# Opening a fused multiply and GELU on its large rows: one load queue, rows of 63 and 60 KB

## The chip, the cores and the metric

The kernel runs on one NeuronCore of a Trainium2 chip. A core has compute engines with an instruction stream each (here VectorE and ScalarE compute, SyncE and ScalarE issue transfers), an on-chip memory of 128 partitions, and 16 DMA engines that move data between that memory and DRAM. The metric is the device time of one execution in microseconds; lower is better.

## The reference

Two float32 arrays of 1024 x 4096 are multiplied, and the tanh form of GELU is taken of the product:

```
z = x * y
return (0.5 * z * (1 + np.tanh(np.sqrt(2 / np.pi) * (z + 0.044715 * z ** 3))))
```

Every element is read once from each of x and y and written once to the output: 3 x 16.78 MB.

## The kernel before

The work is elementwise, so the arrays are taken flat. 4,194,304 elements are 128 partitions x 32768 columns of float32. PIECES cuts the columns into three: [0, 1280), [1280, 17664) and [17664, 32768), which are rows of 5 KB, 64 KB and 59 KB in each partition. A piece is one contiguous stretch of DRAM, and each partition's row is a contiguous part of that stretch (`columns`). Each array so moves in three transfers of 128 rows, 8 rows to each of the 16 DMA engines.

x is loaded into `xs`, which has room for all of it. y is loaded into `ys`, which has room for 20440 columns; Y_LOADS lists y's loads in order, with the column of `ys` where each begins. The second load writes over part of the first one's place, so it waits until three multiplies are done (Y_FREE); the third waits for four.

VectorE multiplies in place, xs = xs * ys, in steps of at most 4096 columns (STEPS); ScalarE then applies GELU in place to the same columns. `sem_mul` and `sem_act` count their steps. Pieces are computed in the order 64 KB, 59 KB, 5 KB, and stored in the same order, each by one transfer once ScalarE is through with it. The first store also waits until y's second load has landed.

All orders are written out by hand. SyncE issues all transfers but one, in program order, and waits in between; each engine that issues has its own DMA queue (q1 is SyncE's, q10 ScalarE's). `_hoist` moves an issue ahead of the program's common start, so that it goes out at once. Before the change two loads are hoisted: x's 5 KB rows on SyncE and x's 64 KB rows on ScalarE. SyncE then waits for the 5 KB rows to land (line 81) before it issues y's 64 KB rows and x's 59 KB rows; ScalarE waits for them too (line 89) before it begins its part.

Of the kernel before, what the change touches and what calls it, by code (L numbers as in the profile page):

```python
# [1 line left out]

# [4 lines left out]


F32 = mybir.dt.float32
GELU = mybir.ActivationFunctionType.Gelu_apprx_tanh  # L10

PIECES = [(0, 1280), (1280, 17664), (17664, 32768)]

Y_LOADS = [(1280, 17664, 4056), (17664, 32768, 0), (0, 1280, 15104)]

Y_FREE = [0, 3, 4]

STEPS = [[4096] * 4, [2048] * 7 + [768], [1280]]  # L20
STORES = [(1280, 17664), (17664, 32768), (0, 1280)]
Y_BUF = 20440


def _hoist(nc, issued):

    here = nc.cur_bb.bb.instructions
    first = nc.main_func.blocks[0].instructions
    for ins in issued:
        del here[next(k for k, i in enumerate(here) if i is ins or i.name == ins.name)]  # L30
    engine = issued[0].engine
    at = next(
        k
        for k, i in enumerate(first)
        if i.engine == engine and type(i).__name__ == "InstDrain"
    )
    first[at:at] = issued


@with_exitstack  # L40
def kernel(
    ctx: ExitStack,
    tc: tile.TileContext,
    x: bass.AP,
    y: bass.AP,
    out: bass.AP,
):
    nc = tc.nc
    P = nc.NUM_PARTITIONS

    def columns(t, a, b):

        flat = t.flatten_outer_dims().rearrange("r c -> (r c)")
        pa, pb = next(q for q in PIECES if q[0] <= a and b <= q[1])
        return flat[P * pa : P * pb].rearrange("(p c) -> p c", p=P)[:, a - pa : b - pa]


    tc.close()
    tc.compile()

    xs = nc.alloc_sbuf_tensor("xs", [P, PIECES[-1][1]], F32).ap()
    ys = nc.alloc_sbuf_tensor("ys", [P, Y_BUF], F32).ap()
    sem_x = [nc.alloc_semaphore(f"sem_x{i}") for i in range(len(PIECES))]
    sem_y = [nc.alloc_semaphore(f"sem_y{i}") for i in range(len(Y_LOADS))]
    sem_mul = nc.alloc_semaphore("sem_mul")
    sem_act = nc.alloc_semaphore("sem_act")
    sem_o = [nc.alloc_semaphore(f"sem_o{i}") for i in range(len(STORES))]

    def load_x(i, engine=nc.sync):
        a, b = PIECES[i]  # L70
        return engine.dma_start(out=xs[:, a:b], in_=columns(x, a, b)).then_inc(sem_x[i], 16)

    def load_y(i):
        a, b, r = Y_LOADS[i]
        return nc.sync.dma_start(
            out=ys[:, r : r + b - a], in_=columns(y, a, b)
        ).then_inc(sem_y[i], 16)

    _hoist(nc, [load_x(0).ins])
    _hoist(nc, [load_x(1, nc.scalar).ins])  # L80
    nc.sync.wait_ge(sem_x[0], 16)
    load_y(0)
    load_x(2)
    for i in range(1, len(Y_LOADS)):
        if Y_FREE[i]:
            nc.sync.wait_ge(sem_mul, Y_FREE[i])
        load_y(i)

    nc.scalar.wait_ge(sem_x[0], 16)
    n = 0  # L90
    done = {}
    for i, (a, b, r) in enumerate(Y_LOADS):
        for j, (xa, xb) in enumerate(PIECES):
            if xa <= a < xb:
                nc.vector.wait_ge(sem_x[j], 16)
        nc.vector.wait_ge(sem_y[i], 16)  # L96
        c = a
        for w in STEPS[i]:
            nc.vector.tensor_mul(  # L99
                out=xs[:, c : c + w],  # L100
                in0=xs[:, c : c + w],
                in1=ys[:, r + c - a : r + c - a + w],
            ).then_inc(sem_mul, 1)
            n += 1
            done[c + w] = n
            nc.scalar.wait_ge(sem_mul, n)
            nc.scalar.activation(  # L107
                out=xs[:, c : c + w], in_=xs[:, c : c + w], func=GELU
            ).then_inc(sem_act, 1)
            c += w  # L110

    for i, (a, b) in enumerate(STORES):
        if i == 0:
            nc.sync.wait_ge(sem_y[-2], 16)
        nc.sync.wait_ge(sem_act, done[b])
        nc.sync.dma_start(out=columns(out, a, b), in_=xs[:, a:b]).then_inc(sem_o[i], 16)
    for i in range(len(STORES) - 1):
        nc.sync.wait_ge(sem_o[i], 16)
    nums = sorted(s.num for s in [*sem_x, *sem_y, *sem_o[:-1], sem_mul, sem_act])
    assert nums == list(range(nums[0], nums[-1] + 1))  # L120
    nc.sync.sem_clear(range(nums[0], nums[-1] + 1))
    nc.sync.wait_ge(sem_o[-1], 16).then_inc(sem_o[-1], -16)


# [1 line left out]
_INS = ['x', 'y']  # L126
_OUTS = [((1024, 4096), 'float32')]


# [23 lines left out]
```

## Time and profile before

| what | value |
|---|---|
| median of 3 runs | 119.9 us (119.77 to 119.95) |
| the profiled execution: its span, from first to last instruction | 118.5 us (a time of its own beside the span is not recorded) |
| VectorE busy, 13 multiplies | 35.2 us (30%) |
| ScalarE busy, 13 activations and a table load | 30.9 us (26%) |
| packets of the DMA engines, q1 and q10 | 82.3% and 16.5% of the 16 engines' span |
| x's 5 KB rows: issued at, time to landing | 0.00 us, 13.6 us (SyncE) |
| x's 64 KB rows | 0.12 us, 30.4 us (ScalarE) |
| y's 64 KB rows | 13.57 us, 29.0 us |
| x's 59 KB rows | 13.96 us, 46.5 us |
| y's 59 KB rows | 55.79 us, 22.5 us |
| stores of 64, 59 and 5 KB rows: time to landing | 20.9, 20.4 and 20.8 us |

The DMA share of a stretch is the mean busy share of the 16 DMA engines, from the durations of their packets; a packet counts in the stretch where it begins, so a short stretch can show more than 1. One row is one packet, and each transfer adds 16 small ones that signal its completion. The chain that ended last follows the work back from the last instruction, at each step to what released it. A transfer's time to landing includes its time in the queue behind others.

### The profile page before, as it was taken

The numbers are of one execution on the slowest core, as the hardware profiler recorded it, in microseconds if no ns is written. First come the engines' busy times: TensorE is split into PE (matmuls) and PEld (weight loads), VectorE is DVE, ScalarE is ACT, GpSimd is POOL, SyncE is SP. The second block draws the span as 40 slices with busy tenths as digits, with TensorE's granted clock in tenths as the row PEclk, the third lists the DMA queues.
The fourth block names the chain that finished last, engine by engine and source line by source line (L and its number), as shares of the span: only waits on it lengthen the run. The fifth ranks groups of instructions, "written<-read, shape, count | busy, mean of one in ns | idle before, by whom it ended". The sixth has DMA issues, their size and how long they took to land.

```text
span 118.5 us, 83 instructions
## 1 busy us (share of the span) xinstructions
DVE 35.2 (30%) x13; ACT 30.9 (26%) x14; POOL 0.2 (0%) x4
## 2 busy tenths in 40 slices
DVE  0000000000000069999920000059999940000000
ACT  0000000000000000999975000006998990000000
POOL 0000000000000000000000000000000000000000
DMA  9888899889988897798797797798899887977975
GB/s 492 382 382 382 354 597 464 354 354 465 597 354 354 354 632 347 326 632 347 326 632 347 326 632 347 326 575 354 354 531 531 354 354 326 653 326 326 653 326 221
DMA packets 1296, 50.33 MB, mean 425 GB/s; under 512 B 144, under 2 KB 144, under 8 KB 528
## 3 DMA queue, kind: packets, MB, share of 16 engines
q1 hardware_dynamic: 1152, 41.94, 82.3%
q10 hardware_dynamic: 144, 8.39, 16.5%
HBM read 33.55 MB, written 16.78 MB: 425 GB/s over the span
## 4 chain that ended last, share of the span: by engine, by line
DMA 55%; DVE 24%; ACT 3%; issue 1%; DVEq 0%
DMA ys<-in_y_dram 43%; DVE xs L99 24%; DMA xs<-in_x_dram 11%; ACT xs L107 3%; DVEq L96 0%
## 5 line engine op out<-in xcount | busy, mean ns | idle before, releaser
L99 DVE TENSOR_TENSOR xs<-xs,ys 128x2048 f32<-128x2048 f32 (+3 forms) x13 | 35.2, 2778 | 60.9 <-DMA ys<-in_y_dram 60.9
L107 ACT ACTIVATE xs<-xs 128x2048 f32<-128x2048 f32 (+3 forms) x13 | 29.6, 2300 | 19.6 <-DVE xs L99 19.6
L107 ACT ACT_TABLE_LOAD x1 | 1.3, 1283 | 47.2 <-DVE xs L99 47.2
L137 POOL MEMSET const-uint8-127<- 128x1 uint8 x1 | 0.1, 102 | 0.0
L137 POOL MEMSET const-bfloat16-1.0<- 128x1 bf16 x1 | 0.1, 101 | 0.0
L137 POOL MEMSET const-float32-0.0<- 128x1 f32 x1 | 0.1, 98 | 0.2 <-issue 0.2
L137 POOL MEMSET const-float32-1.0<- 128x1 f32 x1 | 0.1, 98 | 0.0
## 6 DMA issues: line engine op xcount, KB each, us to landing
xs<-in_x_dram SPq DMA_DIRECT2D x1, 7552.0 KB, 46.5
ys<-in_y_dram SPq DMA_DIRECT2D x1, 7552.0 KB, 22.5
out_dram<-xs SPq DMA_DIRECT2D x1, 7552.0 KB, 20.4
xs<-in_x_dram SPq DMA_DIRECT2D x1, 640.0 KB, 13.6
ys<-in_y_dram SPq DMA_DIRECT2D x1, 640.0 KB, 19.7
out_dram<-xs SPq DMA_DIRECT2D x1, 640.0 KB, 20.8
xs<-in_x_dram ACTq DMA_DIRECT2D x1, 30.4
ys<-in_y_dram SPq DMA_DIRECT2D x1, 29.0
```

What stands on the lines that cost most here:

```text
L99: nc.vector.tensor_mul(out=xs[:, c : c + w], in0=xs[:, c : c + w], in1=ys[:, r + c - a : r + c - a + w],).then_inc(sem_mul, 1)
L107: nc.scalar.activation(out=xs[:, c : c + w], in_=xs[:, c : c + w], func=GELU).then_inc(sem_act, 1)
L137: nc = _bacc.Bacc("TRN2", target_bir_lowering=False, num_devices=1)
```

## The change

The cut between the two large pieces moves from column 17664 to 17408: rows of 63 KB and 60 KB take the place of 64 KB and 59 KB, in loads, steps and stores. The second load of y still waits for three multiplies. The first piece's last step becomes 3840 columns; the second piece's last step of 768 becomes two, 640 and 384.

Only x's 63 KB rows are hoisted, on SyncE. ScalarE issues no transfer any more. SyncE does not wait before y's first load: behind the hoisted load it issues y's 63 KB rows, x's 60 KB rows and x's 5 KB rows. ScalarE waits for x's 63 KB rows where it waited for the 5 KB rows.

```
-PIECES = [(0, 1280), (1280, 17664), (17664, 32768)]
+PIECES = [(0, 1280), (1280, 17408), (17408, 32768)]
 
-Y_LOADS = [(1280, 17664, 4056), (17664, 32768, 0), (0, 1280, 15104)]
+Y_LOADS = [(1280, 17408, 4312), (17408, 32768, 0), (0, 1280, 15360)]
 
 Y_FREE = [0, 3, 4]
 
-STEPS = [[4096] * 4, [2048] * 7 + [768], [1280]]
-STORES = [(1280, 17664), (17664, 32768), (0, 1280)]
+STEPS = [[4096] * 3 + [3840], [2048] * 7 + [640, 384], [1280]]
+STORES = [(1280, 17408), (17408, 32768), (0, 1280)]
...
-    _hoist(nc, [load_x(0).ins])
-    _hoist(nc, [load_x(1, nc.scalar).ins])
-    nc.sync.wait_ge(sem_x[0], 16)
+    _hoist(nc, [load_x(1).ins])
     load_y(0)
     load_x(2)
+    load_x(0)
     for i in range(1, len(Y_LOADS)):
         if Y_FREE[i]:
             nc.sync.wait_ge(sem_mul, Y_FREE[i])
         load_y(i)
 
-    nc.scalar.wait_ge(sem_x[0], 16)
+    nc.scalar.wait_ge(sem_x[1], 16)
```

## The prediction

> **What bounds the kernel now.** I read the page's DMA rows first, then the chain that ended last, then the DMA queues over short stretches, then SyncE's waits.
>
> ```profile
> span 118.5 us, 83 instructions
> ...
> DVE 35.2 (30%) x13; ACT 30.9 (26%) x14; POOL 0.2 (0%) x4
> ...
> DMA packets 1296, 50.33 MB, mean 425 GB/s; under 512 B 144, under 2 KB 144, under 8 KB 528
> ...
> q1 hardware_dynamic: 1152, 41.94, 82.3%
> q10 hardware_dynamic: 144, 8.39, 16.5%
> ```
>
> The two queues add to 98.8% of 16 engines' span: the 16 DMA engines work for 117.1 of 118.5 us, VectorE and ScalarE for less than a third. So the transfers are the bound, and compute matters only where a transfer waits for it. The bytes, the 1152 rows and the 144 completion packets (9 transfers x 16) stay the same after the change. What is left to win or lose is engine time outside the steady rate, and that I look for by stretches. The next four fences are the DMA view over 3 to 11, 100 to 116, 0 to 2 and 0 to 3 us (packets, MB, share of 16 engines).
>
> ```profile
> q10 hardware_dynamic: 48, 3.15, 90.7%
> q1 hardware_dynamic: 48, 0.25, 7.6%
> ```
>
> ```profile
> q1 hardware_dynamic: 112, 6.77, 97.7%
> ```
>
> ```profile
> q1 hardware_dynamic: 54, 0.28, 49.0%
> ```
>
> ```profile
> q10 hardware_dynamic: 16, 1.05, 85.9%
> q1 hardware_dynamic: 80, 0.41, 43.3%
> ```
>
> Steady: a 64 KB row takes 0.907 x 8 us x 16 / 48 = 2.419 us (27.09 KB/us, with 65.536 KB), a 59 KB row 0.977 x 16 x 16 / 112 = 2.233 us (27.06 KB/us), a 5 KB row 0.076 x 8 x 16 / 48 = 0.20 us. So time goes by bytes, and row length costs nothing that shows. Opening: a 5 KB row takes 0.433 x 3 x 16 / 80 = 0.260 us and the first sixteen 64 KB rows 0.859 x 3 x 16 / 16 = 2.577 us. Over the steady rows that is 80 x 0.060 / 16 = 0.30 us, and 16 x 0.158 / 16 = 0.16 us, of every engine: 0.46 us together. And before any row:
>
> ```profile
> 0.00:1.00 1.00, 0.00 (x0) 0.00 (x0) 0.20 (x4) 1.00 0.00 0
> 1.00:2.00 1.00, 0.00 (x0) 0.00 (x0) 0.00 (x0) 1.00 0.98 276
> ```
>
> Nothing moves in the first 1.0 us (last column, GB/s); in the second the engines are busy (0.98) but move 276 GB/s, not some 430. The opening is the one place where busy engines are slow. The chain and SyncE's waits tell where the transfers depend on compute:
>
> ```profile
> 0.00 13.56 DMA xs<-in_x_dram
> ...
> 13.57 28.99 DMA ys<-in_y_dram
> ...
> 42.66 13.11 DVE xs L99 x3
> ...
> 55.79 22.46 DMA ys<-in_y_dram
> ...
> 78.34 1.52 DVE xs L99
> ...
> 80.55 13.31 DVE xs L99 x6
> ...
> 93.88 3.80 ACT xs L107 x3
> ```
>
> ```profile
> SPq L75 <- DVE xs L99: 45.4, 2, 41.4
> ...
> SPq L116 <- ACT xs L107: 18.7, 2, 17.9
> SPq L116 <- DMA ys<-in_y_dram: 14.5, 1, 14.5
> ```
>
> These waits are not engine idle time: while SyncE waits, earlier transfers run. The third y transfer covers the turn from loads to stores.
>
> **The change part by part.**
>
> *Row lengths.* 63 KB costs 2.419 x 63/64 = 2.381 us, 60 KB 2.233 x 60/59 = 2.271 us. Per engine and array: 8 x (2.381 + 2.271) = 37.22 now, 8 x (2.419 + 2.233) = 37.22 before. Zero.
>
> *Order and queue of the loads.* Before, 640 KB of x on SyncE's queue and 64 KB rows on ScalarE's interleave from about 2 us on. After, one queue holds x's 63 KB rows, y's 63 KB rows, x's 60 KB rows, x's 5 KB rows. A single queue loses nothing in the steady stretch: the 59 KB rows of 100 to 116 us are on one queue and go at full rate.
>
> *SyncE's wait for x's first piece (12.1 us) goes.* y's first load is issued at about 1.4 us instead of 13.57. Late next would be the queue's next transfer, and it isn't: before, 64 KB rows of x ran until 30.5 us (0.12 + 30.4), so y's issue was covered by 17 us; now it is covered by 8 x 2.38 = 19 us. An issue takes 0.33 to 0.43 us in the timeline; four in a row on SyncE end some 1.5 us after they begin, behind those 19 us, so zero; uncovered, the issue moved from ScalarE would cost its 0.36 us. The Trainium skill speaks against merging here (DMA: Bandwidth & Descriptors, Issuing engines are not separate DMA queues): issuing from several engines saves the sequencer's issue time, and nothing else. The saving given up is those 0.36 us and by this trace they lie under 19 us of rows, so by the rule and by the rows the sum is the same.
>
> *ScalarE now waits for x's 63 KB piece.* That lands near 20.5 us; behind the wait stand the table load and the first activation, which need the first multiply (47.17 us before). Zero.
>
> *The opening.* It now has no 5 KB rows. The 0.30 us of their slowness goes; unknown is what the first 63 KB rows cost cold. Low end: nothing above steady (gain 0.46). High end: both costs fall on the first row, and on the slowest engine, which sets each landing (in the trace's packet records single 5 KB rows reach 0.756 us against 0.196, single 64 KB ones 2.858 against 2.418, so 0.56 + 0.44 = 1.0 us, where the mean is 0.46): a loss of up to 0.5. I take the 0.16 us that the first 64 KB rows showed themselves, the same kind of transfer and nearest in time. Gain 0.30 us. The first data are put at 1.0 us after the issue, as now. High end for that: in the stretches above, the 64 KB rows of ScalarE's queue, issued at 0.12 us, have not begun at 2.0 us and all sixteen begin before 3.0. I take 1.0, because the store of 64 KB rows on SyncE's queue, issued at 78.27, has its first packet record at 79.11, 0.84 us later: large rows as such need no 2 us.
>
> *The second half of the loads.* y's first piece lands at 42.56 - 8 x 0.20 (x's 5 KB rows go behind) - 16 x 0.038 (1 KB less on 16 rows) - 0.30 = 40.05. Three multiplies of 13.11 us in total end at 53.3, and SyncE issues y's second load. The queue then still holds x's 60 KB and 5 KB rows until 40.05 + 8 x 2.271 + 1.6 = 59.8: 6.5 us of cover (before 55.8 against 60.4, 4.6). The third y load waits for the fourth multiply (3840 wide, about 4.1 us): 57.4, covered too.
>
> *The steps of the second piece.* 768 becomes 640 + 384: 256 more columns and one more instruction. From the rows 128x4096 (4420 ns) and 128x2048 (2286 ns) VectorE takes 1.042 ns a column; the pitch of 2.20 us between 2048-wide steps leaves 66 ns fixed. 640 + 384 take 1.20 us for 0.87. ScalarE (3612 and 1910 ns) follows: its last step is done 0.35 us later, and the second store is issued at 96.9 instead of 96.55 (both less the gain). The first store's rows end at about 98.5 on the earliest engine (packet records), less 0.3 for 63 KB; 96.9 + 0.84 = 97.74 is before 98.2. Hidden by 0.4 to 0.7 us; uncovered, it costs at most the 0.35.
>
> **Sum.** 118.5 - 0.30 = 118.2 us of span. The median of the runs, 119.9, stands 1.4 us above the span, which shows nothing of it; I keep it: 119.6 us (-0.25%).
>
> **The rivals.**
> 1. *The opening cost belongs to the moment, not to the rows:* until about 2.4 us the memory path is slow whatever it moves. For it: both the 5 KB and the first 64 KB rows are slow, and after that nothing is, not even y's first rows. Against: some 64 KB rows began at the steady 2.418. Then 0.46 stays: 119.9.
> 2. *Slower: large rows open badly.* The 5 KB rows are a cheap warm-up; the first 63 KB row of the latest engine takes both cold costs, and every landing waits for that engine. From where its lag exceeds today's it decides: +0.25 to +0.5, 120.15 to 120.4. Or the first data come at 2.1 us as ScalarE's rows did: +1.1 - 0.3 = +0.8, 120.7. For it: those 2 us; against: the store's 0.84 us.
> 3. *Faster by more:* the opening is at the steady rate and the engines start level: -0.46 to -0.7, 119.2 to 119.4. For it: y's first rows in the load phase show no excess. The Trainium skill (same page, Latency and other measured facts) tells of large power-of-two row pitches in HBM that cost rate, tabulated from 512 KiB up; leaving 64 KB would then help throughout. The trace does not agree: 27.09 against 27.06 KB/us for 64 and 59 KB rows.
> 4. *The second store is late,* if a step on ScalarE costs 0.5 us more than worked out: at most +0.35 on a gain of 0.30: 119.95.
>
> **How the numbers follow.** The runs spread 119.77 to 119.95, so 0.2% (0.24 us) is about what can be told. Forecast 0.48 (0.38 of it past -0.2%, 0.10 short of it); rival 1 0.17, no difference; rival 2 0.23, slower; rival 3 0.09, faster; rival 4 0.03, no difference. Faster 0.47, same 0.30, slower 0.23. The range runs from 119.2 (rival 3's lower part left out) to 120.3 (the late first data left out); the forecast's own is 119.4 to 119.75.
>
> **What would show it.** In the profile after: in the DMA view of the first 3 us only q1, no 5 KB rows, 16 to 32 rows; their mean against 2.381 us is the cold cost (forecast 0.16, rival 1 0.46, rival 2 more). No packet before 1.0 us, and the first soon after. y's first landing near 40.05, its second near 77.95, stores of 20.8 us to landing, the second store's issue before 97.3 and no slack before its rows. A steady row off 27.1 KB/us, or an engine idle between 53 and 60 or at 98 us, makes the prediction wrong.

## The result and the profile after

The changed kernel takes 120.37 us (median of 5 runs, 120.28 to 120.44) against 119.78 us (5 runs beside them; the 119.9 that the forecast starts from is the median of three). The ratio is 1.0047, with a 95% interval of 1.0036 to 1.0059: slower by about half a per cent. The forecast was 119.6 us, faster, with a range up to 120.3. Rival 2, slower because large rows open badly, had named 120.15 to 120.4.

The profiled execution took 120.29 us, and its span is 119.0 us; 1.3 us lie around the span, as before. From the page after, the span and the DMA rows:

```profile
span 119.0 us, 85 instructions
...
DMA packets 1296, 50.33 MB, mean 423 GB/s; under 512 B 144, under 2 KB 144, under 8 KB 528
...
q1 hardware_dynamic: 1296, 50.33, 98.5%
```

Packets and bytes are the same, all on one queue, and the engines are busy for nearly the same share (98.8% before) of a span that is 0.5 us longer. The chain that ended last (start, duration, what) tells by when that half microsecond is lost:

```profile
1.45 39.36 DMA ys<-in_y_dram
...
40.91 13.11 DVE xs L98 x3
...
54.04 24.66 DMA ys<-in_y_dram
...
94.33 4.11 ACT xs L106 x4
```

y's second load lands at 54.04 + 24.66 = 78.70, against 78.25 before: 0.45 us late. y's first lands at 1.45 + 39.36 = 40.81. Without any change of the opening it would have landed at 42.56 - 1.60 - 0.61 = 40.35 (x's 5 KB rows moved behind it, 1 KB less on 16 rows), so there too it is 0.46 late. The whole loss is there by then, and what follows only carries it along. The opening, in the DMA view of 0 to 3 us (packets, MB, share of 16 engines):

```profile
q1 hardware_dynamic: 16, 1.03, 101.2%
```

and, for a steady row, the same view from 4.8 to 20 us:

```profile
q1 hardware_dynamic: 96, 6.19, 94.0%
```

A first row takes 1.012 x 3 x 16 / 16 = 3.036 us; a steady one 0.940 x 15.2 x 16 / 96 = 2.381 us, to the nanosecond what was worked out. So the first row of an engine costs on average 0.655 us more than its bytes. From the second row on there is no excess (2.384 us, packet records). Before, the 5 KB rows and first 64 KB rows together cost 0.46, so the rows themselves make 0.20 of the loss.

Most of the rest is that the engines begin later. In the packet records the first packet stands at 1.02 us, as before. But the 16 engines begin their first rows between 1.02 and 2.04, on average at 1.28; before, all of them had begun by about 1.3, on average at about 1.11. (The records do not name the engine; which packet follows which is read from their times.) That is about 0.17 us. What is left, some 0.1, lies between the engines' mean and the landing. That a landing waits for the latest engine explains little of the loss: from the first engine to the last, y's first piece ends within 0.69 us after the change (39.74 to 40.43) and within 0.68 before (41.55 to 42.23).

### The profile page after: what moved, and what is told of

Its sections match the earlier page's. It is cut to its first block, busy times and chain, and to the rows that moved or that the text cites. A ratio compares the mean times of both kernels' runs of the same rounds, so it can differ in the third digit from the quotient of the medians.

```text
span 119.0 us, 85 instructions
## 1 busy us (share of the span) xinstructions
DVE 35.3 (30%) x14; ACT 31.0 (26%) x15; POOL 0.2 (0%) x4
## 2 busy tenths in 40 slices
DMA packets 1296, 50.33 MB, mean 423 GB/s; under 512 B 144, under 2 KB 144, under 8 KB 528
## 3 DMA queue, kind: packets, MB, share of 16 engines
q1 hardware_dynamic: 1296, 50.33, 98.5%
## 4 chain that ended last, share of the span: by engine, by line
DMA 54%; DVE 23%; ACT 3%; issue 1%; DVEq 0%
DMA ys<-in_y_dram 54%; DVE xs L98 23%; ACT xs L106 3%; DVEq L95 0%
## 5 line engine op out<-in xcount | busy, mean ns | idle before, releaser
L98 DVE TENSOR_TENSOR xs<-xs,ys 128x2048 f32<-128x2048 f32 (+5 forms) x14 | 35.3, 2591 | 61.6 <-DMA ys<-in_y_dram 61.6
L106 ACT ACTIVATE xs<-xs 128x2048 f32<-128x2048 f32 (+5 forms) x14 | 29.7, 2149 | 22.0 <-DVE xs L98 22.0
```

Source lines behind the costliest of these rows:

```text
L98: nc.vector.tensor_mul(out=xs[:, c : c + w], in0=xs[:, c : c + w], in1=ys[:, r + c - a : r + c - a + w],).then_inc(sem_mul, 1)
L106: nc.scalar.activation(out=xs[:, c : c + w], in_=xs[:, c : c + w], func=GELU).then_inc(sem_act, 1)
```

## Experiments: which part of the change costs

Each run is compared with runs of the kernel before on the same chip; ratios are to it. From group to group the kernel before took 119.74 to 119.92 us, so across groups the ratios compare better than the times. Three theories: the opening costs (theory 1, by the size of its rows or by the lack of a second queue), or the row lengths do.

**The old opening with the new cut.**

```
-    _hoist(nc, [load_x(1).ins])
+    _hoist(nc, [load_x(0).ins])
+    _hoist(nc, [load_x(1, nc.scalar).ins])
+    nc.sync.wait_ge(sem_x[0], 16)
...
-    load_x(0)
...
-    nc.scalar.wait_ge(sem_x[1], 16)
+    nc.scalar.wait_ge(sem_x[0], 16)
```

> The opening of before (5 KB rows of x on SyncE, large rows of x on ScalarE, SyncE's wait) with the new cut of 63 and 60 KB. Theory 1, the opening alone makes the difference: the time of before, 119.8 us (119.65 to 119.95), first sixteen large rows near 2.54 us. Rival, row lengths or the split last step cost it: about 120.35 us, with steady rows off 27.1 KB/us or the second store late.

119.83 us, ratio 1.0006 (0.9997 to 1.0014): no difference from before. Cut, split step and stores cost nothing; the first sixteen 63 KB rows, behind the 5 KB rows, take 0.810 x 3 = 2.43 us, less than the 2.54 expected. The DMA view of 0 to 3 us:

```profile
q10 hardware_dynamic: 16, 1.03, 81.0%
```

**The new opening with the old cut.**

```
-PIECES = [(0, 1280), (1280, 17408), (17408, 32768)]
+PIECES = [(0, 1280), (1280, 17664), (17664, 32768)]
...
-STEPS = [[4096] * 3 + [3840], [2048] * 7 + [640, 384], [1280]]
+STEPS = [[4096] * 4, [2048] * 7 + [768], [1280]]
```

(Y_LOADS and STORES go with it.)

> The opening and the single load queue of after, with the cut of before (64 and 59 KB). Theory 1: as slow as after, 120.35 us (120.2 to 120.5), first sixteen rows near 3.0 us against 2.42 steady. Rival (row lengths): 119.8 us.

120.17 us, ratio 1.0033 (1.0020 to 1.0046): slow, though 0.03 under the expected stretch. The first sixteen rows take 1.015 x 3 = 3.045 us against 2.42. The opening makes the difference. The same view:

```profile
q1 hardware_dynamic: 16, 1.05, 101.5%
```

**Small rows first, on one queue** (e3 in later expectations).

```
-    _hoist(nc, [load_x(1).ins])
+    _hoist(nc, [load_x(0).ins, load_x(1).ins])
...
-    load_x(0)
```

> After, with x's 5 KB rows issued ahead of its 63 KB rows, both on SyncE: small rows first, but one queue and no wait. Theory 1a, the size of the first rows costs: 119.8 us or a little less (119.6 to 119.9), first 5 KB rows near 0.26 us, first 63 KB rows near 2.5. Theory 1b, the missing second queue costs (ScalarE's queue): about 120.3 us, with the excess of the first 63 KB rows near 0.6 us.

119.66 us, ratio 0.9993 (0.9984 to 1.0002). The first 63 KB rows take 2.425 us behind the 5 KB rows (packet records). So neither the second queue nor SyncE's wait was worth anything that shows; the order is what counts. The Trainium skill (DMA: Bandwidth & Descriptors, Issuing engines are not separate DMA queues) says that issuing from several engines only saves issue time. The runs agree: with the same cut, two queues take 119.83 and one 119.66 us.

**Large rows first, from ScalarE.**

```
-    _hoist(nc, [load_x(1).ins])
+    _hoist(nc, [load_x(1, nc.scalar).ins])
```

> After, with the opening 63 KB rows issued by ScalarE instead of SyncE, which issues all the rest: two queues, large rows first. Theory 1a (size of the first rows): 120.35 us (120.2 to 120.6), first sixteen rows near 3.0 us. Theory 1b (queue): 119.8 us. If ScalarE's queue itself begins late, as its rows did before (no packet by 2.0 us): about 1 us more than after, 121.3 us.

120.56 us, ratio 1.0065 (1.0052 to 1.0077). First rows of 3.16 us: another queue opens no better. Its first packet comes at 1.14 us, so ScalarE's queue is not late by itself. Before, with the 5 KB load issued 0.12 us ahead of it, its rows began only at 2.23 us; why was not tried.

## Experiments: what about the first rows costs

**5 KB rows that lie 63 KB apart.** `load_part(i, c0, c1)` loads columns c0 to c1 of piece i.

```
-    _hoist(nc, [load_x(1).ins])
+    _hoist(nc, [load_part(1, 0, 1280).ins, load_part(1, 1280, 16128).ins])
```

> After, with the 63 KB rows opened by their first 5 KB (128 rows of 5 KB, 63 KB apart in DRAM) and the other 58 KB behind, all on SyncE. Theory S (the size of the rows that are begun cold costs): as with x's own 5 KB rows first, 119.7 us (119.55 to 119.9), 5 KB rows near 0.24 us. Rival P (the place: rows 63 KB apart spread the cold start over 8 MB, x's own 5 KB rows lie together in 640 KB): 120.2 to 120.4 us, with 5 KB rows well over 0.3 us.

120.03 us, ratio 1.0016 (1.0007 to 1.0026): between the two theories. (The profiled execution was the longest of its nine, 120.35 us.) The DMA view of the first 2 us shows it better; first this run, then the run with x's own 5 KB rows first, on one queue:

```profile
q1 hardware_dynamic: 27, 0.14, 43.4%
```

```profile
q1 hardware_dynamic: 66, 0.34, 48.5%
```

A 5 KB row takes 0.434 x 2 x 16 / 27 = 0.51 us when the rows lie 63 KB apart, and 0.485 x 2 x 16 / 66 = 0.24 us when they lie one behind the other. Same size, other place. Size alone cannot be the cause. The first sixteen far rows take 0.68 us, 0.49 over steady; the 58 KB rows that follow them on busy engines are steady at 2.19 (packet records).

**512 B rows first** (e6 in later expectations).

```
-    _hoist(nc, [load_x(1).ins])
+    _hoist(nc, [load_part(0, 0, 128).ins, load_x(1).ins])
...
-    load_x(0)
+    load_part(0, 128, 1280)
```

> After, with 512 B rows (the first 128 columns of x's 5 KB rows) issued ahead of the 63 KB rows on SyncE. Theory W (each engine's first packet pays once for waking up, whatever its size, so a tiny one pays cheaply): 119.7 us, first 63 KB rows under 2.45 us. Theory T (for some 1 us after its first data the path is slow, and a large row begun in that time loses more than small ones do): the tiny rows are through too soon, 120.0 to 120.3 us, first 63 KB rows 2.7 us or more.

120.78 us, ratio 1.0075 (1.0061 to 1.0089), slower than the change itself (1.0047). The tiny rows take 0.03 us and protect nothing: the 63 KB rows behind them, begun at 1.5 to 2.7 us, take 3.22 us (packet records). The last tiny packet ends at 1.57 us, so most engines are idle again before their 63 KB row. That an engine pays once for waking up, with its first packet, is not so, or it does not outlast this idle time; theory W falls as written. Theory T's bound for the first rows holds, but its time was too low by 0.5.

**The opening in two parts, 16 KB first.**

```
-    _hoist(nc, [load_x(1).ins])
+    _hoist(nc, [load_part(1, 0, 4096).ins, load_part(1, 4096, 16128).ins])
```

> After, with the 63 KB rows opened by their first 16 KB and the other 47 KB behind, on SyncE. A 16 KB row takes 0.60 us when steady, so each engine begins two of them in the first microsecond. If the loss grows with row size: between 119.75 and 120.2 us. If any row well under 63 KB does as well as 5 KB: 119.7. If place decides (rival P): 120.3.

119.96 us, ratio 1.0012 (1.0003 to 1.0021). The first sixteen 16 KB rows take 1.17 us against 0.61 steady: 0.56 over, for a quarter of the bytes, where whole 63 KB rows are 0.66 over. The excess is nearly the same for 5 (0.49), 16 and 63 KB rows at the same places; it isn't proportional to size. So the time lies in the stretch of the first theory, but the rows do not bear it out, and rival P's 120.3 is missed by 0.34. At nearly the same excess the time is less than with whole 63 KB rows while the engines keep closer together: they end y's first piece at 39.92 us on average (40.00 after), but the latest at 40.18 (40.43).

**The opening not hoisted.**

```
-    _hoist(nc, [load_x(1).ins])
+    load_x(1)
```

> After, with the opening load issued at its place in the program, about 1.4 us later, not hoisted. If the slow path belongs to the first use of it: all of the 1.4 us is added, 121.7 us, and the first sixteen 63 KB rows still take about 3.0 us. If it belongs to the time since the program's start (the path is up by about 2.4 us whoever uses it): the first rows are steady, 2.4 us, and the time is 121.0 to 121.2.

121.85 us, ratio 1.0169 (1.0155 to 1.0183). The first rows begin at 2.4 to 2.9 us and take 1.063 x 3 = 3.19 us, by the DMA view of 0 to 3 us:

```profile
q1 hardware_dynamic: 16, 1.03, 106.3%
```

The cost goes with the first use, not with the time since the program's start. That was the prediction's rival 1, and it falls.

**Large rows that lie 5 KB apart.** `load_near(i, pitch)` reads piece i's rows from the start of x, `pitch` elements apart.

```
-    _hoist(nc, [load_x(1).ins])
+    _hoist(nc, [load_near(1, 1280).ins])
```

> After, with the opening 63 KB rows read from places 5 KB apart, overlapping, all within 700 KB of x, instead of 63 KB apart over 8 MB. It moves the same bytes, but the middle columns of x get the wrong data, so this part of the product is not computed. Theory P (place: the first touch of stretches that lie far apart costs each engine): first sixteen rows 2.5 us or less, 119.6 to 119.85 us. Theory S (large rows are slow when begun cold, wherever they lie): first sixteen rows near 3.0 us, 120.2 to 120.5 us. If reading the same bytes from several engines slows the later rows too, steady rows over 2.39 us will show it.

119.82 us, ratio 0.9995 (0.9986 to 1.0004): 63 KB rows first, nothing ahead, and no slower than before. In the DMA view of 0 to 3 us of this run

```profile
q1 hardware_dynamic: 16, 1.03, 89.5%
```

is 0.895 x 3 x 16 / 16 = 2.685 us a row, 0.35 less than after. Second rows are 0.11 over steady on average (up to 0.28), later ones almost none. All engines begin by 1.30 us, as they did before and not after. The expected 2.5 us was missed, the time was hit. The four openings side by side, as ratios to before:

| | rows one near the other (5 KB apart) | rows 63 KB apart |
|---|---|---|
| 5 KB rows first | 0.9993 | 1.0016 |
| 63 KB rows first | 0.9995 | 1.0047 |

In time, where the rows lie makes the first difference, and size shows only for rows far apart. (The upper right run has one transfer more than the others.)

**2.5 KB rows first.**

```
-    _hoist(nc, [load_x(1).ins])
+    _hoist(nc, [load_part(0, 0, 640).ins, load_x(1).ins])
...
-    load_x(0)
+    load_part(0, 640, 1280)
```

> After, with half of x's 5 KB rows (2.5 KB rows, 5 KB apart) ahead of the 63 KB rows on SyncE, the other half behind. Eight of them are about 0.85 us of work for each engine, against 1.6 us for 5 KB rows and 0.2 to 0.3 us for the 512 B rows. Theory H (the first touch of the far stretches takes a fixed time of about 1 us per engine and is begun early, behind whatever work is queued ahead, so the excess that shows is what this work doesn't cover: 0.84 us behind 0.25, 0.05 behind 1.6): first 63 KB rows 2.5 to 2.8 us, 119.9 to 120.3 us. Rival T (what decides is that no large row begins in the first us): first rows begin near 2 us; by e6, whose rows that began at 2.3 and 2.7 us still took 2.75 us, they would take 2.75 or more: 120.4 or more.

120.17 us, ratio 1.0023 (1.0012 to 1.0034). The 63 KB rows behind take 2.55 us, 0.17 over steady. With 512 B rows ahead it was 0.84, with 5 KB rows 0.045: the more work is queued ahead, the less of the cost shows, as theory H says. Rival T's 2.75 did not come.

**512 B rows at the far places first.**

```
-    _hoist(nc, [load_x(1).ins])
+    _hoist(nc, [load_part(1, 0, 128).ins, load_part(1, 128, 16128).ins])
```

> After, with the first 512 B of each 63 KB row ahead of the other 62.5 KB, on SyncE. Theory P/H (first touch of the place): the tiny rows take the cost, their first ones 0.4 us or more each, the 62.5 KB rows behind run near their steady 2.36 us, 119.9 to 120.4 us in all. Theory S (size): the tiny rows are quick as in e6 (0.03 us), the large ones behind cost 0.6 to 0.9 us over steady, 120.5 to 120.9 us.

120.81 us, ratio 1.0070 (1.0056 to 1.0084). The tiny rows again take 0.03 us, and the 62.5 KB rows behind them 3.23 us against 2.36. This was a miss for theories P and H as written: reading the first 512 B of each far row beforehand doesn't pay the cost of the row. A first touch of the place where a row begins is not what costs. As with 512 B rows of x's first piece, the tiny rows are through (1.56 us) before most of the large ones begin (1.52 to 2.29).

**Small rows first on one queue, old cut.** The edit of the small-first run on the cut of before.

> Small rows first on one queue, as e3, with the cut of before (64 and 59 KB). If the cut costs nothing: as e3, 119.66 us (119.55 to 119.8), at or just under before. If the 64 KB rows do better or worse behind 5 KB rows in one queue: off that by over 0.15 us.

119.75 us, ratio 0.9986 (0.9977 to 0.9995), so 0.05 to 0.23% under before. Its interval lies under 1, by a margin that hardly counts, and under that of the change (1.0036 to 1.0059). With the new cut the same order came to 0.9993, and its interval includes 1. The first 64 KB rows take 2.53 us here, 0.11 over steady, so what is left of the cost behind 5 KB rows is not always as little as 0.045.

**Small rows landed, then large ones.** Still open: do the near rows bring the path up, or do they only cover the cost, that is, keep it from showing while they are queued ahead?

```
-    _hoist(nc, [load_x(1).ins])
+    _hoist(nc, [load_x(0).ins])
+    nc.sync.wait_ge(sem_x[0], 16)
+    load_x(1)
     load_y(0)
     load_x(2)
-    load_x(0)
```

> After, with x's 5 KB rows hoisted, and SyncE waiting until they have landed before it issues the 63 KB rows: near rows first as in e3, but nothing of the far rows can be begun behind them, and the engines stand idle in between for some 1.5 us. Theory U (the near rows bring the path up, and it stays up): first sixteen 63 KB rows 2.40 to 2.48 us; with the idle time 121.0 to 121.6 us. Theory H (the cost of the far rows is only covered by queued work): they take about 3.0 us again, 121.8 to 122.3 us.

122.32 us, ratio 2.1% over before (1.0196 to 1.0230), at the upper end of what theory H gave. In the DMA view of 4 to 6 us

```profile
q1 hardware_dynamic: 16, 1.03, 153.8%
```

the first 63 KB rows take 1.538 x 2 x 16 / 16 = 3.076 us, as if nothing had gone before. The last of the 5 KB rows had ended 1.3 us before the first of them began, at 4.59 us (packet records), and the engines were idle in between (the stretch of 3 to 4 us: DMA share 0.02):

```profile
3.00:4.00 1.00, 0.00 (x0) 0.00 (x0) 0.00 (x0) 1.00 0.02 5
```

The 640 KB that had landed brought nothing up that outlasts this idle time: theory U falls. The same 5 KB rows, still queued ahead, leave 0.045 us of the cost. What stands of theory H is that work queued ahead keeps the cost from showing; its first touch of far stretches fell with the 512 B rows at the far places. Whether the cost is hidden behind that work, or does not arise on engines that are already at work, these runs do not tell apart.

**Large rows 16 and 32 KB apart.** `load_near(1, 4096)` and `load_near(1, 8192)`.

> As the run with 63 KB rows 5 KB apart, but 16 KB apart (2.1 MB in all, overlapping; the middle columns get wrong data). If the loss grows with how far apart the rows lie: first sixteen rows between 2.69 us (5 KB apart) and 3.04 us (63 KB apart), near 2.75 to 2.85 us, 119.85 to 120.1 us. If only overlapping reads made that run quick: here too 2.69 us, as the rows still overlap four times.

> The same with rows 32 KB apart (4.2 MB in all, each byte read about twice). By distance: 2.85 to 3.0 us for the first sixteen rows, 120.0 to 120.3 us.

120.60 us (1.0055 to 1.0085) and 120.20 us (1.0022 to 1.0049). First rows in the view of 0 to 3 us, 16 KB apart and then 32 KB apart:

```profile
q1 hardware_dynamic: 16, 1.03, 109.7%
```

```profile
q1 hardware_dynamic: 16, 1.03, 102.8%
```

3.29 and 3.08 us. With the 2.69 at 5 KB and the 3.04 at 63 KB, rows 16 KB apart do no better than rows 32 or 63 KB apart: distance does not decide, and reads that overlap two or four times don't make rows quick either. (At 5 KB apart they overlap some twelve times; whether that helps there is not tried.) That 5 KB apart is good and 16 to 63 KB bad stands; which property of the addresses makes it so stays open.

## Why the prediction was wrong

- **What bounds the kernel:** right. The loss is 0.46 us by y's first landing and 0.45 at its second; the span is 0.5 longer.
- **Row lengths at zero:** right, by the old opening with the new cut (1.0006) and by the steady row of 2.381 us.
- **One queue, and SyncE's wait and issue moved, at zero:** right, by small rows first on one queue (0.9993).
- **ScalarE's wait at zero:** right; the table load still stands behind the first multiply.
- **First data at 1.0 us:** right for the first packet, 1.02. But the engines begin about 0.17 us later on average than before (1.28 for 1.11), which the sum did not have. The 2 us of ScalarE's rows were no property of large rows or of that queue (1.14 when it opens).
- **The opening at -0.30:** the step that failed; it measured +0.46. The 5 KB rows' 0.30 did go. But the new first rows were priced at the 0.16 that the old first 64 KB rows showed, as "the same kind of transfer". Those rows had five or so 5 KB rows ahead of them on every engine. Behind 5 KB rows in the queue the runs show 0.05 to 0.16 of the cost; with nothing ahead it is 0.66, and 0.70 even when 5 KB rows had landed before. So the first row alone was 0.50 too cheap; with the later begin (0.17) and some 0.1 between the engines' mean and the landing this makes up the 0.76 from -0.30 to +0.46. The term was taken from a row whose cost did not show, and the same edit took away the rows that kept it from showing. The prediction's high end, a loss of up to 0.5, held it, and the range should have reached there. What in the far rows costs stays open.
- **y's second load covered by 6.5 us:** right. It was issued at 54.04, and the queue's work lasted until 60.1 (packet records).
- **The second store:** right. The timeline has its issue at 97.30, 0.75 later than before: 0.45 lost at the opening and 0.30 of the split step, forecast at 0.35. The first store's rows ended at 98.67 at the earliest, and no engine went idle there.
- **Rival 1** (the moment): fell with the opening not hoisted. **Rival 2** (slower): right in sign, and 120.37 lies in its stretch, at the upper end. Its picture of one latest engine was wrong: the cost is 0.66 on the mean of all sixteen. Nor are the 5 KB rows a warm-up that lasts: 1.3 us of idle engines later nothing of it is left. **Rival 3** (large power of two): no sign of it; 64 KB rows opened no worse than 63 KB rows (3.045 and 3.036 us). **Rival 4** (the second store late) did not come.

## What to carry to other kernels

A duration read from a row is the cost of that operation behind the work that stood ahead of it; when the edit takes that work away, price the operation without it, or keep the high end in the range. In a kernel bound by transfers, look at the first microseconds by packets: here a small load of neighbouring rows, queued ahead of the large one, kept 0.6 us from showing that the large one costs when it goes first. It had to stand in the queue ahead; landed beforehand, with 1.3 us of idle engines between, it did nothing, and rows of 512 B were too short.

## What the runs showed of the hardware

- A load of 63 or 64 KB rows that starts on idle engines lost 0.63 to 0.91 us per engine in its first rows when they lay 16 to 64 KB apart, and 0.3 when they lay 5 KB apart (2.69 against 2.38 us). Rows of 5 and 16 KB that lay 63 KB apart lost 0.49 and 0.56. Rows of 512 B showed none of it, at either place.
- The cost comes again after 1.3 us of idle engines (3.08 us), and not at a change to other far stretches with work queued ahead (y's first rows behind x's: 2.38 us).
- One queue alone carried all 50.33 MB with the engines busy for 98.5% of the span, at 27.1 KB/us for each of the 16 engines.
